# Four edits to a two-layer encoder on one core: ring tiles for the first weights behind the product pairs, later loads of stored tiles, another order inside each pair, a priority for the additions

## The chip, the core and the metric

The kernel runs on one core of a Trainium2 chip. The core's engines are named as in the profile: PE (TensorE, matmuls), DVE (VectorE), ACT (ScalarE), POOL (GpSimd) and SP (SyncE, which only issues transfers). The metric is the device time of one execution in microseconds (us); the times are medians over several runs.

## The reference

Two layers work on a sequence of 512 tokens with 16 meta tokens put ahead of them, 528 rows (`T`) of 2048 features, all in fp32. The first layer mixes by grouped-query softmax attention, the second by gated linear attention (GLA) in chunks, in both directions. Each has a gate path, and norms on both sides:

```
h = concat([meta, x])
for i in range(2):
    y = rmsnorm(h, pre_norm[i])
    y = attention_mixer(y, ...) if i == 0 else gla_mixer(y, ...)   # ends in (o * silu(gate)) @ w_out
    h = h + rmsnorm(y, post_norm[i])
return h[:, 16:]
```

Most of the arithmetic is in products with weights: `w_in` of the attention layer (2048 x 6144), its `w_out` (2048 x 2048), and the same two of the GLA layer.

## The kernel before

**Layout.** Activations lie with features on the 128 partitions and tokens along the free axis: 16 tiles (`KT`) of 128 features by 528 tokens. An output tile is 128 columns of a weight matrix by 528 tokens, computed as two halves of 264 tokens (`HALF`). An fp32 product is made of three: each operand is split into a high part (a cast) and a low part (what is left), and high x high, high x low and low x high are added up in PSUM (`three`, L152 to L155). The activations' parts are `uh` and `ul`.

**Weights.** `weights` (L141) loads a unit of 1024 columns (8 k tiles of 128 x 128) into a raw tile `wraw`, of which there are two, by SP's queue (L148). `split` then casts it on ACT (L130) and subtracts on DVE (L131) into a pair of tiles `whi` and `wlo`, a ring of three. A call may bring its own pair of tiles instead (`own`). `project` (L157) multiplies two such units, 48 matmuls for each half tile, and hands the bank to an `evac` function.

**Pairs.** `seven` (L213) computes two output tiles together with seven products instead of eight, in Strassen's manner: the weights for two tiles are a 2 x 2 block of quarters a11, a12, a21, a22 (1024 columns each, loaded at L219 by SP's queue), and the activations were combined ahead into `th`, `tl` (by `combine`) with four columns T1 to T4. Each product is 24 matmuls (L239 to L241). Sums of quarters are made on DVE (L232), every operand is split into ring tiles (`parts`), results are copied from PSUM on ACT (L268, L270, L272, L280) and partial results are added to what is there on DVE (`add`, L247). Six raw tiles pass through a list `free`: the two `wraw` and four others; a pair returns the list in the order in which the next shall use it. Pairs make up the attention gates (5 pairs, in 106 to 215 us), eight tiles of the attention's output product (4 pairs, in 813 to 895 us) and the GLA values (6 pairs, in 1042 to 1173 us).

**Behind the output product's pairs.** The output tiles 0 to 12 are stored to `y_d` as they come. When the last pair is done, its pools are closed, and a pool `tp` takes their space: in it lie the 16 tiles `hs`, the three pairs `own`, and tiles for a small product of the next layer (`wr`, loaded at L856, and `wl`, which is cleared on POOL at L858 and cast from `wr` on ACT). POOL issues the loads of 13 stored tiles (L851). Then come the last three output tiles, 13, 14 and 15 (`TAIL`): first the left half of each, then the right half, with the same split weights (`kept`, six units: tile 13 with k 0 to 7, tile 13 with k 8 to 15, then 14 and 15 likewise). The first three units go to `own` tiles, the last three to the ring. `squares` copies each half to `hs` (L868), squares it on ACT (L870) and adds the squares up on POOL (L872). From the sums `mean_rsqrt` makes a row, with which `residual` (L893 to L898) makes the next layer's input on DVE and ACT; the first product of the next layer (L982, weights `w_in1`) follows, with transposes of `hs` (L935) between its matmuls.

**What sets the order.** A scheduler puts the instructions on each engine in order, by the order in which they are written and by priorities: a block in `tc.high_priority(n)` counts as written n steps earlier (`AHEAD` for weights and sums, `AHEAD + 200` for the quarters' loads). `clk` is an aid for the writing: `clk.after(dt, fn)` calls `fn` when products worth dt us have been written. It makes nothing wait on the chip. Each engine then runs its list in that order.

Of the kernel before, what the change touches and what calls it, by code (L numbers as in the profile page):

```python
# [11 lines left out]
F32R = mybir.dt.float32r  # L12
I32 = mybir.dt.int32
AF = mybir.ActivationFunctionType
ALU = mybir.AluOpType
# [4 lines left out]
P = 128  # L20
# [14 lines left out]
AHEAD = 400  # L35
# [47 lines left out]
def hybrid_encoder(  # L83
# [5 lines left out]
    nc = tc.nc  # L89
    V, A, G, PE = nc.vector, nc.scalar, nc.gpsimd, nc.tensor  # L90
    clk = Clock()

    def pool(stack, name, bufs=1, **kw):
        return stack.enter_context(tc.tile_pool(name=name, bufs=bufs, reuse_waits="tile", **kw))
# [13 lines left out]
    y_d = scratch.tile([13, P, T], F32, name="y_d")  # L108
# [20 lines left out]
    def split(hi, lo, src):  # L129
        A.copy(hi, src)  # L130
        V.tensor_tensor(lo, src, hi.bitcast(F32), op=ALU.subtract)  # L131
# [10 lines left out]
    def weights(src, ahead=AHEAD, queue=nc.sync, own=None):  # L142
        n = src.shape[-1]
        with tc.high_priority(ahead):
            raw = wpool.tile([P, 1024], F32, tag="wraw", name="wraw", bufs=2)
            hi, lo = own or (wpool.tile([P, 1024], F32R, tag="whi", name="whi"),
                             wpool.tile([P, 1024], F32R, tag="wlo", name="wlo"))
            queue.dma_start(out=raw.rearrange("p (k n) -> p k n", n=n), in_=src)  # L148
            split(hi, lo, raw)
        return hi.rearrange("p (k n) -> p k n", n=n), lo.rearrange("p (k n) -> p k n", n=n)  # L150
# [40 lines left out]
    T1, T3, T4, T2 = range(0, 4 * HALF, HALF)  # L191
# [23 lines left out]
    def seven(src, c, ys, th, tl, free, ps_x):  # L215

        def quarter(t, i, j):
            with tc.high_priority(AHEAD + 200):
                nc.sync.dma_start(out=t.rearrange("p (k n) -> p k n", n=P),  # L219
                                  in_=src[:, j * KH:(j + 1) * KH, c + i * P:c + (i + 1) * P])  # L220
            return t

        def parts(raw):
            with tc.high_priority(AHEAD):
                hi = wpool.tile([P, 1024], F32R, tag="whi", name="whi")
                lo = wpool.tile([P, 1024], F32R, tag="wlo", name="wlo")
                split(hi, lo, raw)
            return [t.rearrange("p (k n) -> p k n", n=P) for t in (hi, lo)]

        def sums(o, a, b, op=ALU.subtract):  # L230
            with tc.high_priority(AHEAD):
                V.tensor_tensor(o, a, b, op=op)  # L232

        def product(w, b, ps=None, more=False):
            if ps is None:
                ps = ps_x.tile([P, 512], F32, tag="x", name="px")[:, :HALF]
            bh, bl = b
            for k in range(KH):
                PE.matmul(ps, w[0][:, k], bh[:, k], start=k == 0 and not more, stop=False, skip_group_check=more)  # L239
                PE.matmul(ps, w[0][:, k], bl[:, k], start=False, stop=False, skip_group_check=more)  # L240
                PE.matmul(ps, w[1][:, k], bh[:, k], start=False, stop=k == KH - 1,  # L241
                          skip_group_check=more)
                clk.step(3 * (HALF + 7) / 2400)
            return ps

        def add(o, ps, y):
            V.tensor_tensor(o, ps, y, op=ALU.add)  # L247

        def of_u(j, n):
            a, b = HALVES[n]  # L250
            return [t[:, j * KH:(j + 1) * KH, a:b] for t in (uh, ul)]

        def of_t(o):
            return [t[:, :, o:o + HALF] for t in (th, tl)]
        a11, a21, a22, s, a12, spare = free
        for t, i, j in ((a11, 0, 0), (a21, 1, 0), (a22, 1, 1), (a12, 0, 1)):
            quarter(t, i, j)
        y1, y2 = ys
        l, r = slice(0, HALF), slice(HALF, T)
        w1 = parts(a11)  # L260
        sums(s, a21, a22, ALU.add)
        w5 = parts(s)
        sums(a21, a11, a21)
        sums(a11, s, a11)
        w2 = parts(a11)
        p1 = ps_p.tile([P, 512], F32, tag="pp", name="pp")[:, :HALF]
        product(w1, of_u(0, 0), p1)
        A.copy(y1[:, l], p1)  # L268
        p5 = product(w5, of_t(T1))
        A.copy(y2[:, r], p5)  # L270
        product(w2, of_t(T2), p1, True)
        A.copy(y1[:, r], p1)  # L272
        add(y1[:, l], product(parts(a12), of_u(1, 0)), y1[:, l])
        sums(a11, a12, a11)
        product(parts(a21), of_t(T3), p1, True)
        add(y2[:, r], p1, y2[:, r])
        product(parts(a11), of_u(1, 1), p5, True)
        add(y1[:, r], p5, y1[:, r])
        product(parts(a22), of_t(T4), p1, True)
        A.copy(y2[:, l], p1)  # L280
        return [spare, s, a21, a11, a12, a22]

    w_in0 = attn_w_in[0].rearrange("(k p) n -> p k n", p=P)
    w_out0 = attn_w_out[0].rearrange("(k p) n -> p k n", p=P)
# [262 lines left out]
    for h in range(3):  # L547
        y = yp.tile([P, T], F32, tag=f"y{h % 2}", name="y")
# [258 lines left out]
    def y_tile(i):  # L807
        return yp.tile([P, T], F32, tag=f"y{i}", name=f"y{i}")
# [19 lines left out]
    for m in range(2, 5):  # L828
        y = y_tile(m % 2)
# [17 lines left out]
    tp = pool(tr, "tp")  # L847
    t2 = pool(tr, "t2", 2)
    hs = [tp.tile([P, T], F32, name=f"h{k}") for k in range(KT)]
    for m in range(KT - 3):  # L850
        nc.gpsimd.dma_start(out=hs[m], in_=y_d[m])  # L851
    r0 = tp.tile([P, T], F32, name="r0")


# [86 lines left out]
    turn, spare = [0], [True]  # L941
# [27 lines left out]
                    clk.after(3.2 + t, lambda k=k, t=t: token_major(k - 3, t))  # L969
            yield 0.6  # L970

    own = [[tp.tile([P, 1024], F32R, name=f"own{i}{w}") for w in "hl"] for i in range(3)]
    kept = {}
    for part in HALVES:
        for m in range(KT - TAIL, KT):
            if m not in kept:
                kept[m] = [weights(w_out0[:, k0:k0 + 8, m * P:(m + 1) * P], own=own.pop(0) if own else None)
                           for k0 in (0, 8)]
            project(w_out0, m * P, (part,), evac, ws=kept[m])
    clk.finish(*side)  # L980
# [447 lines left out]
    y = [fp.tile([P, D], F32, name=f"y{t}") for t in range(4)]  # L1428
# [75 lines left out]
```

## Time and profile before

| | |
|---|---|
| median of 3 runs | 1802.85 us (1802.39 to 1803.79) |
| the profiled execution | 1801.52 us |
| its span in the trace | 1799.8 us |
| mean granted clock of TensorE | 0.993 |
| PE busy | 1749.2 us, 97% |
| DVE, ACT, POOL busy | 65%, 54%, 18% |
| PE busy in 106 to 215 us (attention gates) | 105.57 of 109 us |
| PE busy in 813 to 895 us (output pairs) | 82.00 of 82 us |
| PE busy in 895 to 930 us (last three tiles, left and right halves) | 24.58 of 35 us |
| PE busy in 1042 to 1173 us (GLA values) | 128.85 of 131 us |

A window gives, for a stretch of the execution, each engine's busy time and its count of instructions (x), the clock that TensorE was granted, the share of time that the 16 DMA engines were busy, and their rate. A row of a timeline gives the start, the duration, engine, line, operation and tiles, and in brackets the idle time ahead of it with what ended it. All times in the trace are from the start of the span.

### The profile page before, as it was taken

To read this page: it belongs to the slowest core of one execution; us is meant where nothing else is said; L and a number is where in the kernel's file an instruction comes from. 1 tells how busy PE (TensorE), PEld (TensorE's weight loads), DVE (VectorE), ACT (ScalarE), POOL (GpSimd) and SP (SyncE) were. 2 spreads that over 40 slices of the span, in tenths; PEclk is the share of its full clock that TensorE was granted. 3 is DMA by queue.
4 is the path that set the end of the run, shared out by engine and by line. 5 is a ranking of instruction groups with operands and counts; after the bars stand their busy time and mean duration, and the time that the engine had idled before them with its cause. 6 is when DMAs were issued, how large, how long until landed. Compare 5 with 4: busy or idle time off the path is not lost. (4 is left out here: it accounts for less than half of the span.)

```text
span 1799.8 us, 31575 instructions
## 1 busy us (share of the span) xinstructions
PE 1749.2 (97%) x12495; PEld 1647.1 (92%) x12495; DVE 1177.0 (65%) x1913; ACT 978.2 (54%) x1957; POOL 319.5 (18%) x416
## 2 busy tenths in 40 slices
PE   8999999899999999999989999999999999999998
PEld 7999999899999999999989899988898989888886
DVE  4878676666676676776638876668585766764224
ACT  5644455556556455544427544468685765853221
POOL 3124014322422322141221101110000100000000
PEclk9999999999999999999989999999999999999999
DMA  8444423223233233363456444343242332354333
GB/s 251 141 132 122 127 78 101 83 84 107 80 87 101 73 89 107 126 196 113 122 170 207 119 129 119 95 130 107 78 117 72 113 90 85 96 154 176 94 94 129
DMA packets 268068, 211.22 MB, mean 117 GB/s; under 512 B 10284, under 2 KB 240368, under 8 KB 267392
## 3 DMA queue, kind: packets, MB, share of 16 engines
q1 hardware_dynamic: 251600, 159.00, 31.0%
q0 software_dynamic: 16320, 50.21, 8.2%
q8 instruction: 98, 1.61, 0.4%
q14 instruction: 50, 0.41, 0.1%
HBM read 171.15 MB, written 31.52 MB: 113 GB/s over the span
## 5 line engine op out<-in xcount | busy, mean ns | idle before, releaser
L153 PE MATMUL pp<-uh,whi 128*128 128x264 f32 (+1 forms) x2064 | 641.8, 311 | 5.8 <-ACT whi L130 5.2
L155 PE MATMUL pp<-uh,wlo 128*128 128x264 f32 (+1 forms) x2064 | 632.0, 306 | 2.0 <-DVE wlo L131 1.6
L154 PE MATMUL pp<-ul,whi 128*128 128x264 f32 (+1 forms) x2064 | 631.3, 306 | 2.2 <-DVE ul L442 2.2
L131 DVE TENSOR_TENSOR wlo<-wraw,whi 128x1024 fp32r<-128x1024 f32 (+1 forms) x233 | 286.3, 1229 | 245.8 <-ACT whi L130 244.2
L153 PEld LDWEIGHTS pp<-uh,whi 128*128 128x128 f32 x2064 | 390.7, 189 | 22.5 <-ACT whi L130 5.5
L155 PEld LDWEIGHTS pp<-uh,wlo 128*128 128x128 f32 x2064 | 390.6, 189 | 19.6 <-DVE wlo L131 2.4
L154 PEld LDWEIGHTS pp<-ul,whi 128*128 128x128 f32 x2064 | 391.4, 190 | 16.0 <-DVE ul L442 2.6
L130 ACT CAST whi<-wraw 128x1024 fp32r<-128x1024 f32 (+1 forms) x233 | 242.6, 1042 | 274.1 <-PE f L1416 83.4
L130 ACT CAST whi<-x 128x1024 fp32r<-128x1024 f32 x57 | 59.8, 1049 | 71.3 <-PE pp L240 25.4
L131 DVE TENSOR_TENSOR wlo<-x,whi 128x1024 fp32r<-128x1024 f32 x57 | 73.5, 1290 | 35.3 <-ACT whi L130 35.3
L310 POOL DMA_DIRECT2D qs<-qw x96 | 48.3, 508 | 252.1 <-ACT sq L304 215.7
L662 ACT ACTIVATE pn<-s,mx 128x528 f32<-128x528 f32 (+1 forms) x72 | 50.1, 696 | 48.6 <-DVE mx L659 48.6
L1416 PE MATMUL f<-whi,ul 128*128 128x512 f32 x192 | 75.6, 394 | 0.0
L1414 PE MATMUL f<-whi,uh 128*128 128x512 f32 x192 | 75.5, 393 | 0.0
L1415 PE MATMUL f<-wlo,uh 128*128 128x512 f32 x192 | 75.3, 392 | 0.0
L659 DVE TENSOR_REDUCE mx<-s 128x1 f32<-128x528 f32 (+1 forms) x72 | 50.6, 703 | 28.0 <-PE s L656 27.4
L239 PE MATMUL px<-uh,whi 128*128 128x264 f32 x240 | 68.4, 285 | 0.0
L241 PE MATMUL px<-uh,wlo 128*128 128x264 f32 x240 | 68.3, 284 | 0.0
L240 PE MATMUL px<-ul,whi 128*128 128x264 f32 x240 | 67.9, 283 | 0.0
L677 DVE TENSOR_TENSOR pl<-pT,ph 128x512 fp32r<-128x512 f32 (+1 forms) x80 | 47.3, 591 | 18.9 <-ACT ph L676 18.3
L676 ACT CAST ph<-pT 128x512 fp32r<-128x512 f32 (+1 forms) x80 | 40.8, 509 | 31.0 <-PE pT L672 24.9
L1260 POOL DMA_DIRECT2D og_d<-og x24 | 12.9, 542 | 186.2 <-DVE og L1258 186.2
(472 smaller groups left out, 4253.1 us busy)
## 6 DMA issues: line engine op xcount, KB each, us to landing
wraw<-in_attn_w_in_dram SPq DMA_DIRECT2D x80, 512.0 KB, 4.0
wraw<-in_gla_w_in_dram SPq DMA_DIRECT2D x80, 512.0 KB, 4.0
wraw<-in_gla_w_out_dram SPq DMA_DIRECT2D x32, 512.0 KB, 3.9
wraw<-in_attn_w_out_dram SPq DMA_DIRECT2D x22, 512.0 KB, 4.1
x<-in_gla_w_in_dram SPq DMA_DIRECT2D x16, 512.0 KB, 4.2
x<-in_attn_w_in_dram SPq DMA_DIRECT2D x14, 512.0 KB, 4.3
qs<-qw POOLq DMA_DIRECT2D x96, 66.0 KB, 4.0
x<-h_d SPq DMA_DIRECT2D x32, 132.0 KB, 2.9
```

What stands on the lines that cost most here:

```text
L130: A.copy(hi, src)
L131: V.tensor_tensor(lo, src, hi.bitcast(F32), op=ALU.subtract)
L153: PE.matmul(ps, wh, uh[:, k, a:b], start=first, stop=False)
L154: PE.matmul(ps, wh, ul[:, k, a:b], start=False, stop=False)
L155: PE.matmul(ps, wl, uh[:, k, a:b], start=False, stop=last)
L239: PE.matmul(ps, w[0][:, k], bh[:, k], start=k == 0 and not more, stop=False, skip_group_check=more)
L240: PE.matmul(ps, w[0][:, k], bl[:, k], start=False, stop=False, skip_group_check=more)
L241: PE.matmul(ps, w[1][:, k], bh[:, k], start=False, stop=k == KH - 1, skip_group_check=more)
L659: V.reduce_max(mx, s, axis=AX.XY, negate=True)
L1414: PE.matmul(ps, uh[:, k, ts], wh[:, kk], start=(k == 0), stop=False)
L1415: PE.matmul(ps, uh[:, k, ts], wl[:, kk], start=False, stop=False)
L1416: PE.matmul(ps, ul[:, k, ts], wh[:, kk], start=False, stop=(k == KT - 1))
```

## The change: what it does

1. `add` (L247) runs in `tc.high_priority(AHEAD + 100)`: ahead of splits and sums that are written in the same place, behind the quarters' loads.
2. In `seven` the quarters are loaded in the order a11, a12, a21, a22 (before: a11, a21, a22, a12). The plain product of a12 with `uh` comes second, with its addition right behind it; the product with T1, which opens the bank p5, goes from second to fourth, with its copy. The split of a12 (`w6`) stands right behind that of a11. The list for the next pair is returned in another order.
3. The loads of the 13 stored tiles are no longer written at once but at 6.0 + 1.25 m us of written products.
4. The first three units of the last three tiles use the ring, the last three the `own` tiles.

One line more in `add` moves every later line number up by one.

```
         def add(o, ps, y):
-            V.tensor_tensor(o, ps, y, op=ALU.add)
+            with tc.high_priority(AHEAD + 100):
+                V.tensor_tensor(o, ps, y, op=ALU.add)
...
-        for t, i, j in ((a11, 0, 0), (a21, 1, 0), (a22, 1, 1), (a12, 0, 1)):
+        for t, i, j in ((a11, 0, 0), (a12, 0, 1), (a21, 1, 0), (a22, 1, 1)):
             quarter(t, i, j)
         y1, y2 = ys
         l, r = slice(0, HALF), slice(HALF, T)
         w1 = parts(a11)
+        w6 = parts(a12)
         sums(s, a21, a22, ALU.add)
-        w5 = parts(s)
         sums(a21, a11, a21)
         sums(a11, s, a11)
         w2 = parts(a11)
         p1 = ps_p.tile([P, 512], F32, tag="pp", name="pp")[:, :HALF]
         product(w1, of_u(0, 0), p1)
         A.copy(y1[:, l], p1)
-        p5 = product(w5, of_t(T1))
-        A.copy(y2[:, r], p5)
+        add(y1[:, l], product(w6, of_u(1, 0)), y1[:, l])
         product(w2, of_t(T2), p1, True)
         A.copy(y1[:, r], p1)
-        add(y1[:, l], product(parts(a12), of_u(1, 0)), y1[:, l])
+        p5 = product(parts(s), of_t(T1))
+        A.copy(y2[:, r], p5)
         sums(a11, a12, a11)
         product(parts(a21), of_t(T3), p1, True)
...
-        return [spare, s, a21, a11, a12, a22]
+        return [spare, a21, a12, a11, s, a22]
...
     for m in range(KT - 3):
-        nc.gpsimd.dma_start(out=hs[m], in_=y_d[m])
+        clk.after(6.0 + 1.25 * m, lambda m=m: nc.gpsimd.dma_start(out=hs[m], in_=y_d[m]))
...
-    own = [[tp.tile([P, 1024], F32R, name=f"own{i}{w}") for w in "hl"] for i in range(3)]
+    own = [None] * 3 + [[tp.tile([P, 1024], F32R, name=f"own{i}{w}") for w in "hl"] for i in range(3)]
...
-                kept[m] = [weights(w_out0[:, k0:k0 + 8, m * P:(m + 1) * P], own=own.pop(0) if own else None)
+                kept[m] = [weights(w_out0[:, k0:k0 + 8, m * P:(m + 1) * P], own=own.pop(0))
```

How the order moves is seen in the engines' lists. First ACT, from the end of the last pair of the output product on: `y` are the pair's results, `whi` ring tiles, `h` and `sq` the evacuation of a half tile. Before:

```order
L280 COPY y_10706<-pp 128x264
L816 ACTIVATE sq<-y_10706 128x528
L130 CAST own0h<-wraw 128x1024
L130 CAST own1h<-wraw 128x1024
L130 CAST own2h<-wraw 128x1024
L130 CAST whi<-wraw 128x1024
L868 COPY h_10950<-pp 128x264
L870 ACTIVATE sq<-pp 128x264
L130 CAST whi<-wraw 128x1024 x2
L868 COPY h_10951<-pp 128x264
L130 CAST wl<-wr 128x16x16 x2
```

The same place after the change:

```order
L130 CAST whi<-wraw 128x1024 x2
L817 ACTIVATE sq<-y_10705 128x528
L130 CAST whi<-wraw 128x1024
L281 COPY y_10706<-pp 128x264
L817 ACTIVATE sq<-y_10706 128x528
L130 CAST own0h<-wraw 128x1024
L130 CAST own1h<-wraw 128x1024
L130 CAST wl<-wr 128x16x16 x2
L869 COPY h_10950<-pp 128x264
L871 ACTIVATE sq<-pp 128x264
L130 CAST own2h<-wraw 128x1024
```

Three casts of the tail's weights now stand ahead of the last pair's last copy (L281), and the two casts of `wl` have moved ahead of the first half tile's evacuation and of the cast for own2.

POOL at the same place, from the last addition of the pairs' squares on, before (`h_10937` to `h_10949` are the 13 stored tiles; ten of the rows are left out here):

```order
L817 TENSOR_TENSOR acc<-acc,sq 128x528
L851 DMA h_10937<-y_d 128x528
L851 DMA h_10938<-y_d 128x528
...
L851 DMA h_10949<-y_d 128x528
L856 DMA wr<-in_gla_w_in_dram 128x16x32
L858 MEMSET wl 128x2048
L872 TENSOR_TENSOR acc<-acc,sq 128x264 x4
```

After, with rows left out in the same way:

```order
L818 TENSOR_TENSOR acc<-acc,sq 128x528
L857 DMA wr<-in_gla_w_in_dram 128x16x32
L859 MEMSET wl 128x2048
L852 DMA h_10937<-y_d 128x528
L852 DMA h_10938<-y_d 128x528
L852 DMA h_10939<-y_d 128x528
L873 TENSOR_TENSOR acc<-acc,sq 128x264
L852 DMA h_10940<-y_d 128x528
...
L852 DMA h_10944<-y_d 128x528
L873 TENSOR_TENSOR acc<-acc,sq 128x264
L852 DMA h_10945<-y_d 128x528
...
```

The load of `wr` and the clearing of `wl` now come first, and the stored tiles' loads follow in three runs of 3, 5 and 5 with additions between them.

DVE in the second attention pair, whose results are `y_1519` and `y_1520` (`x_751` to `x_754` are raw tiles of the list `free`), before:

```order
L232 TENSOR_TENSOR x_754<-wraw,x_752 128x1024
L247 TENSOR_TENSOR y_1519<-px,y_1519 128x264
L232 TENSOR_TENSOR wraw<-x_751,wraw 128x1024
L131 TENSOR_TENSOR wlo<-wraw,whi 128x1024
L247 TENSOR_TENSOR y_1520<-pp,y_1520 128x264
```

After:

```order
L248 TENSOR_TENSOR y_1519<-px,y_1519 128x264
L131 TENSOR_TENSOR wlo<-wraw,whi 128x1024
L131 TENSOR_TENSOR wlo<-x_754,whi 128x1024
L536 SCALAR_TENSOR_TENSOR sq<-ssq,erow 128x264
L232 TENSOR_TENSOR x_754<-wraw,x_752 128x1024
L232 TENSOR_TENSOR wraw<-x_751,wraw 128x1024
L131 TENSOR_TENSOR wlo<-x_753,whi 128x1024
L248 TENSOR_TENSOR y_1520<-pp,y_1520 128x264
```

The first addition has moved ahead of the next pair's sums by several steps; the second still stands behind two sums and a split. In the first GLA pair, `tl<-x_12144,th`, the low part of the last but one step of `combine`, has moved ahead of one sum and one split of DVE; the tile `x_12144` is the one into which a12 is loaded, before and after.

More of the change, by code (lines that the diff above doesn't have):

```diff
@@ L246, in add @@
         def add(o, ps, y):
-            V.tensor_tensor(o, ps, y, op=ALU.add)
+            with tc.high_priority(AHEAD + 100):
+                V.tensor_tensor(o, ps, y, op=ALU.add)
         def of_u(j, n):
@@ L255, in seven @@
         a11, a21, a22, s, a12, spare = free
-        for t, i, j in ((a11, 0, 0), (a21, 1, 0), (a22, 1, 1), (a12, 0, 1)):
+        for t, i, j in ((a11, 0, 0), (a12, 0, 1), (a21, 1, 0), (a22, 1, 1)):
             quarter(t, i, j)
@@ L260, in seven @@
         w1 = parts(a11)
+        w6 = parts(a12)
         sums(s, a21, a22, ALU.add)
-        w5 = parts(s)
         sums(a21, a11, a21)
@@ L268, in seven @@
         A.copy(y1[:, l], p1)
-        p5 = product(w5, of_t(T1))
-        A.copy(y2[:, r], p5)
+        add(y1[:, l], product(w6, of_u(1, 0)), y1[:, l])
         product(w2, of_t(T2), p1, True)
         A.copy(y1[:, r], p1)
-        add(y1[:, l], product(parts(a12), of_u(1, 0)), y1[:, l])
+        p5 = product(parts(s), of_t(T1))
+        A.copy(y2[:, r], p5)
         sums(a11, a12, a11)
@@ L280, in seven @@
         A.copy(y2[:, l], p1)
-        return [spare, s, a21, a11, a12, a22]
+        return [spare, a21, a12, a11, s, a22]
     w_in0 = attn_w_in[0].rearrange("(k p) n -> p k n", p=P)
@@ L850, in hybrid_encoder @@
     for m in range(KT - 3):
-        nc.gpsimd.dma_start(out=hs[m], in_=y_d[m])
+        clk.after(6.0 + 1.25 * m, lambda m=m: nc.gpsimd.dma_start(out=hs[m], in_=y_d[m]))
     r0 = tp.tile([P, T], F32, name="r0")
@@ L970, in residuals @@
             yield 0.6
-    own = [[tp.tile([P, 1024], F32R, name=f"own{i}{w}") for w in "hl"] for i in range(3)]
+    own = [None] * 3 + [[tp.tile([P, 1024], F32R, name=f"own{i}{w}") for w in "hl"] for i in range(3)]
     kept = {}
@@ L976, in hybrid_encoder @@
             if m not in kept:
-                kept[m] = [weights(w_out0[:, k0:k0 + 8, m * P:(m + 1) * P], own=own.pop(0) if own else None)
+                kept[m] = [weights(w_out0[:, k0:k0 + 8, m * P:(m + 1) * P], own=own.pop(0))
                            for k0 in (0, 8)]
```

## The prediction, made before the changed kernel was run

> **What bounds the kernel now.** I read the page first, then windows of 10 us for TensorE, then its waits, and only at the places with a gap the timelines and the DMA views. The page's head and its row for TensorE:
>
> ```profile
> span 1799.8 us, 31575 instructions
> PE 1749.2 (97%) x12495; PEld 1647.1 (92%) x12495; DVE 1177.0 (65%) x1913; ACT 978.2 (54%) x1957; POOL 319.5 (18%) x416
> ```
>
> PE is the bound, so only its stops and its slow clock can be won; the number of matmuls does not change. The windows (x is the count of matmuls, the last three numbers are granted clock, DMA share, GB/s):
>
> ```profile
> 885.00:895.00 10.00, 10.00 (x85) 10.00 (x84) 3.64 (x5) 1.83 (x3) 1.58 (x2) 1.00 0.42 124
> 895.00:905.00 10.00, 6.75 (x42) 6.33 (x41) 3.18 (x5) 2.90 (x4) 7.45 (x13) 0.83 0.65 198
> 905.00:915.00 10.00, 6.51 (x37) 5.88 (x35) 1.23 (x1) 1.05 (x1) 4.60 (x5) 0.83 1.08 354
> 915.00:925.00 10.00, 6.31 (x35) 6.01 (x36) 3.16 (x3) 4.15 (x8) 1.15 (x1) 0.66 0.50 120
> 909.20:912.60 3.40, 3.40 (x18) 3.40 (x17) 0.00 (x0) 0.00 (x0) 2.98 (x2) 0.50 1.07 344
> 145.00:155.00 10.00, 7.72 (x63) 7.53 (x62) 9.45 (x10) 3.94 (x7) 4.78 (x3) 1.00 0.26 82
> ```
>
> A full window holds 85. From 895 to 925 there are 42 + 37 + 35 = 114 where 255 would fit: 141 matmuls are missing, and at 10/85 us each that is 16.6 us. This is the passage from the last pair to the three half tiles. The table of TensorE's waits (total us, times, longest) names what it waits for there and elsewhere:
>
> ```profile
> PE pp L153 <- ACT whi L130: 5.2, 1, 5.2
> PE pp L239 <- DVE y L247: 2.9, 2, 2.3
> PE px L239 <- ACT th L130: 2.1, 1, 2.1
> PE pp L153 <- ACT own0h L130: 2.1, 1, 2.1
> PE ht L935 <- DVE h L896: 1.3, 2, 1.1
> PE pp L155 <- DVE own0l L131: 1.1, 1, 1.1
> PE pp L155 <- DVE own2l L131: 0.8, 1, 0.8
> PE pp L153 <- ACT own2h L130: 0.7, 1, 0.7
> PE px L241 <- DVE wlo L131: 0.4, 1, 0.4
> ```
>
> The tail's own waits (own0, own2, the single whi) are 5.2 + 2.1 + 1.1 + 0.8 + 0.7 = 9.9 us; the other 6.7 of the 16.6 is mainly matmuls at half clock behind those stops. One such stretch is the 3.4 us row above: 18 matmuls instead of 29 cost 11 x 10/85 = 1.3 us.
>
> **The tail, edits 3 and 4.** ACT's and POOL's timelines and the DMA view of 895 to 920 (queues, then issues with count, KB each, median us to landing):
>
> ```profile
> 896.57 1.03 ACT L130 CAST own0h<-wraw 128x1024 fp32r<-128x1024 f32 x1
> 906.17 1.05 ACT L130 CAST own2h<-wraw 128x1024 fp32r<-128x1024 f32 x1 [7.62 <-DMA wraw<-in_attn_w_out_dram]
> 917.14 1.04 ACT L130 CAST whi<-wraw 128x1024 fp32r<-128x1024 f32 x1 [9.92 <-DMA wraw<-in_attn_w_out_dram]
> 924.62 0.71 ACT L130 CAST wl<-wr 128x256 fp32r<-128x256 f32 x2
> ...
> 896.82 1.31 POOL L817 TENSOR_TENSOR acc<-acc,sq 128x528 f32<-128x528 f32 x1
> 898.07 5.47 POOL L851 DMA_DIRECT2D h<-y_d  x10
> 909.33 1.17 POOL L856 DMA_DIRECT2D wr<-in_gla_w_in_dram  x1 [0.34 <-DMA h<-y_d]
> ...
> q0 software_dynamic: 1234, 4.12, 50.7%
> q1 hardware_dynamic: 3120, 1.57, 23.4%
> ...
> h<-y_d POOLq DMA_DIRECT2D x13, 264.0 KB, 7.7
> wraw<-in_attn_w_out_dram SPq DMA_DIRECT2D x4, 512.0 KB, 8.4
> wr<-in_gla_w_in_dram POOLq DMA_DIRECT2D x1, 256.0 KB, 7.7
> ```
>
> Two things hold the half tiles up. The first unit's cast (own0h) stands behind the last pair's end, as its tile lies in the space that the pair's tiles leave; and ten loads issued in 5.47 us fill the DMA engines, so that weights land in 8.4 us. The page has the quiet value of the same loads, the PE and DVE timelines the pace of the last pair:
>
> ```profile
> wraw<-in_attn_w_out_dram SPq DMA_DIRECT2D x22, 512.0 KB, 4.1
> ...
> 892.46 0.28 PE L239 MATMUL pp<-sh,whi 128*128 128x264 f32 x1
> ...
> 895.24 0.28 PE L241 MATMUL pp<-sh,wlo 128*128 128x264 f32 x1
> ...
> 887.79 1.23 DVE L131 TENSOR_TENSOR wlo<-wraw,whi 128x1024 fp32r<-128x1024 f32 x1 [0.53 <-ACT whi L130]
> ```
>
> The seventh product's 24 matmuls start from 892.46 to 895.24: 0.121 us each, 2.9 a product, so the fifth ends at 889.6, the sixth at 892.5, the seventh at 895.4. A unit of a half tile is also 24 matmuls, so from 895.4 on units are needed every 2.9 us: 895.4, 898.3, 901.2, 904.1, 907.0, 909.9. A split is a cast of 1.05 and a subtraction of 1.23, 2.3 together. With the ring for the first three, unit 1 needs a ring tile (free at 889.6) and is ready near 892. Unit 2's raw tile is free when the subtraction of 887.79 ends, 889.0; with 4.1 it lands at 893.1 and is ready at 895.4, 2.9 early. Unit 3 uses the raw tile of unit 1: issued near 892, landed 896, ready 898.4, 2.8 early. Unit 4 (own0) is issued at 895.4, ready 901.8, 2.3 early; unit 5 (own1) at 898.4, ready 904.8, 2.2 early. Unit 6 (own2) is issued at 901.8 and would be ready at 908.2, but its cast now stands behind the two wl casts and an evacuation's two steps on ACT. POOL issues wr from 898.1 (end of the addition of 896.82) to 899.3; landing in 7.7 gives 907.0, the casts 907.7, the evacuation about 0.8 more, own2h at 908.5 to 909.6 and own2l to 910.8. Its third matmul, the first with the low part, is due at 909.9 + 0.24: a stop of about 0.6. Bounds: none, if wr lands in 4.1 as the quiet loads do; if own2's load takes 8.4, it lands at 910.2 and is ready at 912.5, a stop of 2.4 and one slow stretch of 1.3, 3.7. I take 0.6, since wr's row is its own. Tail: 16.6 - 0.6 = 16.0 gained (12.9 to 16.6). The wl split and the memset, now early on POOL, wait for nothing that PE needs. The thirteen stored tiles leave POOL in runs of 3, 5 and 5 between additions, not singly; the first three run beside the load of own0 or own1, which have 2.2 to spare.
>
> [...]
>
> The clock: after stops of 0.7 and 0.8 the row of 909.2 shows 0.50; in 145 to 155, with a longest stop of 2.3, it stays 1.00. So one stop of 0.6 may or may not cost 1.3; the sum takes nothing, the bound takes it. [...]
>
> **The pairs, edits 1 and 2.** In the second attention pair the seventh product waits for the addition that reads its bank:
>
> ```profile
> 143.84 2.01 DVE L232 TENSOR_TENSOR wraw<-x,wraw 128x1024 f32<-128x1024 f32 x1
> 145.78 2.33 DVE L131 TENSOR_TENSOR wlo<-wraw,whi 128x1024 fp32r<-128x1024 f32 x1
> 148.02 0.42 DVE L247 TENSOR_TENSOR y<-pp,y 128x264 f32<-128x264 f32 x1
> ```
>
> The attention stops are 2.9 + 0.4 = 3.3 us. In the new order the addition still stands behind two sums and one split; only the 0.4 of the plain product's addition has gone from between. The raised priority would win all 3.3 only if loads landed so early that the order did not matter. I take the middle of 0.4 and 3.3: 1.8 gained. The other pairs, but for the first of the GLA layer (below), are not among these waits, so they can only lose; their weights keep coming through the same raw tiles at 4.1, and I take 0.
>
> The first GLA pair has the stop on th (2.1). The plain product needs no th, so this goes; but it needs a12, whose tile the last step of combine frees:
>
> ```profile
> 1041.51 1.26 DVE L131 TENSOR_TENSOR tl<-x,th 128x1056 fp32r<-128x1056 f32 x1
> ...
> 1045.32 0.38 ACT L268 COPY y<-pp 128x264 f32<-128x264 f32 x1 [2.06 <-PE pp L241]
> 1048.53 1.05 ACT L130 CAST whi<-x 128x1024 fp32r<-128x1024 f32 x1 [2.83 <-DMA x<-in_gla_w_in_dram]
> ```
>
> Now the tile is free at 1042.8 and its load ends near 1048.5: 5.7. In the new order that subtraction stands ahead of one sum and one split, 2.3 earlier (1.23 and about 1.05): free at 1040.5, landed at 1044.6 (4.1) to 1046.2 (5.7), split until 1046.9 to 1048.5. The second product is due at 1045.3, its low part at 1045.6: a new stop of 1.3 to 2.9, taken as 2.1. Net 0 (-0.8 to +0.8).
>
> **Behind the tail** the residuals make PE wait 1.3 (ht). With the tail 16 us shorter, two splits of w_in1 (1.23 each on DVE) may fall ahead of that chain: 0 taken, bounds -1.3 to +2.5.
>
> Sum: -16.0 - 1.8 + 0 + 0 = -17.8. The profiled execution took 1801.52 us (span 1799.8), so 1783.7; the median of the runs, 1802.85, is 1.33 above it: **1785.1**. All best ends: -16.6 - 3.3 - 0.8 - 1.3 = -22.0, 1780.9. All worst: -12.9 - 0.4 + 0.8 + 2.5 = -10.0, 1792.9.
>
> **Rivals.** *Weights still crowded* (chance 0.13): all three own loads take 8.4. Own0 lands at 903.8, ready 906.1: 1.7 late; own1 lands 906.8, ready 909.1, 0.4 late; own2 waits for own0's raw tile, issued 906.1, lands 914.5, ready 916.8, 4.5 late. With two slow stretches 1.7 + 0.4 + 4.5 + 2.6 = 9.2 instead of 0.6: 1793.7. For it: the loads of stored tiles still come in runs, and wr joins them. Against: 3 tiles, not 10, stand ahead of own0's landing.
>
> *Given back behind the tail* (0.10): the two splits delay the residuals by 2.5 and the stop slows the clock once, 1.3: +3.8, 1788.9.
>
> *Slower* (0.04): in each of the 15 pairs the addition, now pinned early on DVE, holds back the splits and sums behind it until its product ends, and so the raw tiles and next loads. It turns slower from 17.8/15 = 1.2 us a pair. DVE is busy 65%, 1.9 us of a product's 2.9, so about 1 us a product is to spare; a hold of one product less that, 1.9 a pair, gives 15 x 1.9 - 17.8 = +10.7, 1813.6. Against: additions wait for a product that is next to end anyway, and 885 to 895, the end of a pair, is full with the same three additions in it.
>
> *No change* (0.01): the first half tile stays behind the pair's end because ring and raw tiles come no sooner. The times above speak against it by 2 us.
>
> **How the numbers follow.** The forecast has 0.72, and its two faster rivals 0.23; what a measurement here can tell from no change is 0.2%, 3.6 us, and all three lie further below. Faster 0.95, same 0.01, slower 0.04. The range runs from the best end, 1780, to 1793, which holds the forecast's worst end and the second rival and leaves most of the first outside.
>
> **What would show it.** Right: 895 to 905 holds 85 matmuls, own0h is cast before it is needed, PE has no wait over 1 us on own tiles, and the clock stays 1.00; the next stage starts 16 us sooner. In the first GLA pair the stop moves to the second product. Wrong: loads of weights that take 8 us between 895 and 915, a wait on own2h of several us, or full windows turning to 80 inside the pairs.

## The result and the profile after

The changed kernel takes 1786.34 us (median of 4 runs, 1783.37 to 1787.44) against 1802.62 us for the kernel before (4 runs): the ratio is 0.9911 with a 95% interval of 0.9891 to 0.9931, 16 us less, by the interval 12 to 20. The forecast was 1785.1. The profiled execution took 1787.44 (span 1785.7).

The windows of the changed kernel over the tail, and over the second attention pair, in the columns of those shown of before:

```profile
895.00:905.00 10.00, 10.00 (x84) 10.00 (x84) 7.17 (x6) 4.66 (x7) 7.33 (x7) 1.00 0.81 228
905.00:915.00 10.00, 8.09 (x65) 7.67 (x64) 4.27 (x6) 3.91 (x8) 5.50 (x10) 1.00 0.96 307
915.00:925.00 10.00, 10.00 (x80) 9.87 (x81) 2.32 (x4) 3.12 (x6) 3.01 (x6) 1.00 0.69 231
145.00:155.00 10.00, 8.21 (x55) 8.00 (x54) 9.45 (x10) 3.74 (x6) 4.67 (x4) 0.83 0.26 82
```

From 895 to 925 there are now 84 + 65 + 80 = 229 matmuls where there were 114, and the clock stays at 1.00. One stop is left, in the second row. (The first 2.7 us of the first row still belong to the last pair, which ends at 897.7 now and ended at 895.4 before.) The attention pair's window has become worse: 55 for 63, at a clock of 0.83. TensorE's waits in the whole execution name both:

```profile
PE pp L239 <- DVE y L248: 2.7, 3, 1.8
PE px L241 <- DVE wlo L131: 1.9, 3, 0.8
PE pp L153 <- ACT own2h L130: 1.2, 1, 1.2
PE ht L936 <- DVE h L897: 1.1, 1, 1.1
PE pp L155 <- DVE own2l L131: 0.7, 1, 0.7
```

The waits on own0 (2.1 and 1.1), on the ring tile (5.2) and on th (2.1) are gone. Where the time went is seen from the length of the stages, from the first matmul of a stage to the first of the next (in the pairs, to 0.12 us behind the start of the last matmul), in us, worked out from the starts in the traces:

| kernel | attention pairs | to the output pairs | output pairs | tail, to the first GLA pair | GLA pairs | rest |
|---|---|---|---|---|---|---|
| before | 108.2 | 598.9 | 81.7 | 146.8 | 130.4 | 627.2 |
| the change | 109.9 | 599.3 | 82.6 | 131.9 | 130.0 | 626.2 |
| ring order alone | 107.8 | 600.4 | 82.6 | 139.2 | 130.4 | 627.4 |
| later loads alone | 108.5 | 600.7 | 83.6 | 139.0 | 131.5 | 627.0 |
| both edits of the tail | 108.2 | 602.5 | 81.9 | 130.8 | 130.2 | 627.5 |
| both edits of the pairs | 110.1 | 602.7 | 81.7 | 144.9 | 129.6 | 626.4 |
| the change, fold copied on ACT | 109.3 | 599.0 | 81.7 | 129.5 | 130.0 | 626.5 |
| the change, rotation of the first head group left out | 103.5 | 600.2 | 81.7 | 129.5 | 129.7 | 626.4 |

The second stage, which no edit of the first seven touches, shows how far two profiles differ by themselves: 598.9 to 602.7. Between before and the change the tail gave 14.9 us, the rest behind GLA 1.1 and the GLA pairs 0.4; 0.8 came ahead of the first pair, and attention took back 1.8, the output pairs 1.0 and the stretch between them 0.4: together 14.1, the difference between the two profiled executions.

### The profile page after: what moved, and what is told of

The parts are those of the page before. It is cut to its first block, busy times and chain, and to the rows that moved or that the text cites. A ratio compares the mean times of both kernels' runs of the same rounds, so it can differ in the third digit from the quotient of the medians.

```text
span 1785.7 us, 31568 instructions
## 1 busy us (share of the span) xinstructions
PE 1745.8 (98%) x12495; PEld 1643.6 (92%) x12495; DVE 1182.2 (66%) x1913; ACT 978.6 (55%) x1957; POOL 319.5 (18%) x416
## 4 chain that ended last, share of the span: by engine, by line
PE 69%; DVE 4%; ACT 2%; DMA 2%; issue 1%; POOL 1%; DVEq 0%; ACTq 0%; POOLq 0%; SPq 0%
PE pp L153 12%; PE pp L155 12%; PE pp L154 12%; PE f L1417 2%; PE f L1415 2%; PE f L1416 2%; PE pp L239 2%; PE pp L240 2%; PE pp L241 2%; PE px L241 1%; PE px L239 1%; PE px L240 1%; PE pT L673 1%; DVE wlo L131 1%; DMA wraw<-in_attn_w_out_dram 1%
## 5 line engine op out<-in xcount | busy, mean ns | idle before, releaser
L131 DVE TENSOR_TENSOR wlo<-wraw,whi 128x1024 fp32r<-128x1024 f32 (+1 forms) x230 | 280.4, 1220 | 231.6 <-ACT whi L130 230.0
L241 PEld LDWEIGHTS px<-uh,wlo 128*128 128x128 f32 x240 | 45.1, 188 | 2.5 <-DVE wlo L131 2.5
## 6 DMA issues: line engine op xcount, KB each, us to landing
x<-h_d SPq DMA_DIRECT2D x32, 132.0 KB, 2.8
```

## The experiments

**The tail's two edits, apart and together.** Ring order alone:

```
-    own = [[tp.tile([P, 1024], F32R, name=f"own{i}{w}") for w in "hl"] for i in range(3)]
+    own = [None] * 3 + [[tp.tile([P, 1024], F32R, name=f"own{i}{w}") for w in "hl"] for i in range(3)]
...
-                kept[m] = [weights(w_out0[:, k0:k0 + 8, m * P:(m + 1) * P], own=own.pop(0) if own else None)
+                kept[m] = [weights(w_out0[:, k0:k0 + 8, m * P:(m + 1) * P], own=own.pop(0))
```

> Kernel before with the ring order alone (first three units of the last three tiles in ring tiles, last three in own tiles; the 13 stored tiles still loaded at once). Theory A (ring order and later loads each carry a part): the stop of 2.4 at the pair's end and the 1.4 and slow stretch behind it go (some 5 us), but own tiles loaded among the 13 loads land in 8 us or more, so a wait on own tiles of 4 to 8 us and a slow stretch stay: 6 to 10 us faster than before, near 1794. Rival B (the ring order alone is the gain, the loads do not matter): 15 us faster, no wait over 2 us on own tiles.

Measured: 1796.5 us, ratio 0.9961 (0.9947 to 0.9975). Later loads alone:

```
-        nc.gpsimd.dma_start(out=hs[m], in_=y_d[m])
+        clk.after(6.0 + 1.25 * m, lambda m=m: nc.gpsimd.dma_start(out=hs[m], in_=y_d[m]))
```

> Kernel before with the later loads of the stored tiles alone (own tiles still first). Theory A: the stop at the pair's end (2.4 and 1.4, with a slow stretch of 1.3) stays, the waits on own2 and on the ring tile behind it shrink from 7.5 us to under 2: 8 to 11 us faster, near 1793. Rival B: within 2 us of before. Rival C (crowding is the whole loss): 15 us faster.

Measured: 1797.36 us, ratio 0.9966 (0.9952 to 0.9981). Both:

> Kernel before with both edits of the tail (ring order and later loads), pairs and additions as before. Theory A, from the stages of the two profiles: the tail gains 15 us by itself and the pairs' edits have lost about 2, so this is faster than the full change: 15 to 17 us under before, 1 to 3 us under the full change. Rival D (the pairs' new order is what frees the raw tiles early enough for the ring): 5 us or more of the gain are missing here.

Measured: 1787.7 us, ratio 0.9908 (0.9893 to 0.9923). TensorE's waits from the last pair's end on, first of the ring order alone, then of the later loads alone:

```profile
PE pp L153 <- ACT own2h L130: 6.2, 1, 6.2
PE pp L155 <- DVE own2l L131: 0.4, 1, 0.4
```

```profile
PE pp L153 <- ACT own0h L130: 2.1, 1, 2.1
PE pp L155 <- DVE wlo L131: 1.4, 2, 0.8
PE pp L155 <- DVE own0l L131: 1.1, 1, 1.1
PE pp L155 <- DVE own2l L131: 0.7, 1, 0.7
PE pp L153 <- ACT own2h L130: 0.7, 1, 0.7
```

With both edits the 30 us from the last pair's end hold no stop:

```profile
898.00:928.00 30.00, 30.00 (x246) 29.87 (x245) 13.30 (x20) 12.90 (x23) 15.49 (x21) 1.00 0.86 269
```

Each edit takes away the stops that belong to it: the ring those on own0 at the pair's end, the later loads the long one behind own2. Each shortens the tail by 8 us, and both by 16: the two add up. Theory A holds for the stops and the stages, with the ring order at the edge of its 6 to 10 by the medians (6.3 us) and the later loads below their 8 to 11 (5.5 us); the waits left on own2 and the ring tile there are 2.8 us together and not under 2. Rivals B and C fall. Rival D falls too, since the old pairs feed the ring as well. One part of theory A missed: this kernel was to be 1 to 3 us under the full change, and its ratio of 0.9908 cannot be told from the full change's 0.9911. So by the times edits 1 and 2 add nothing to the two edits of the tail and take nothing from them.

**The pairs' edits by themselves** (the changed kernel with the two edits of the tail undone).

> The full change without the two edits of the tail: pairs in the new order and additions first, the last three tiles and the loads as before. Theory A: 0 to 3 us slower than before: attention pairs up to 2 slower by a stop and a slow stretch, output pairs 1 slower, first GLA pair 0.5 faster. Rival D: 3 us or more faster, as forecast for attention or more.

Measured: 1801.11 us, ratio 0.9988 (0.9979 to 0.9997), 0.5 to 3.8 us faster, where theory A had 0 to 3 slower. Rival D misses too. The profiled execution is the longest of the eleven (1804.37) and 2.9 longer than that of before; 3.8 more went into the stretch between attention and output pairs, which the edits do not touch. Its stages show a loss and a gain: attention is slower, 110.1 against 108.2, as with all edits, while the GLA pairs and what is behind them are 1.6 faster. Another 1.9 lies in the tail, where this kernel's loads are those of before; whether that comes of the pairs' order is not shown, as a later kernel with the old pairs and the old tail (rotation on DVE, below) has 1.0 less than before there as well. Edit 1 has no part in it by itself: in the kernel before, with that edit alone, every engine's order is as it was, since the additions did not stand where a priority moves them.

**The stop that was left on own2.** In the changed kernel DVE, POOL, ACT and SP show these rows around it:

```profile
900.57 4.33 DVE L866 COPY fold<-ident 64x64 f32<-64x64 f32 x2
905.05 1.23 DVE L131 TENSOR_TENSOR own0l<-wraw,own0h 128x1024 fp32r<-128x1024 f32 x1
...
900.55 1.32 POOL L818 TENSOR_TENSOR acc<-acc,sq 128x528 f32<-128x528 f32 x1
901.83 1.19 POOL L857 DMA_DIRECT2D wr<-in_gla_w_in_dram  x1
903.01 1.83 POOL L859 MEMSET wl<- 128x2048 f32 x1
...
902.09 1.05 ACT L130 CAST own0h<-wraw 128x1024 fp32r<-128x1024 f32 x1 [1.69 <-DMA wraw<-in_attn_w_out_dram]
906.73 0.72 ACT L130 CAST wl<-wr 128x256 fp32r<-128x256 f32 x2 [0.71 <-DMA wr<-in_gla_w_in_dram]
912.48 1.04 ACT L130 CAST own2h<-wraw 128x1024 fp32r<-128x1024 f32 x1 [4.47 <-DMA wraw<-in_attn_w_out_dram]
...
906.30 0.37 SPq L148 DMA_DIRECT2D wraw<-in_attn_w_out_dram  x1
```

ACT's cast of own2 waited for its load, not for the casts of wl, which were done 5 us earlier. The load was issued at 906.30, when own0's subtraction had freed the raw tile; and that subtraction, whose cast was done at 903.1, stood until 905.05 behind two copies of 64 x 64 that took 4.33 us. They end where POOL's clearing ends (904.90 and 904.84). The load itself took 6.2 us, where those of own0 and own1 took 4.3. An estimate from these rows: with the subtraction right behind its cast, or with a landing in 4.1, 0.3 or less of the 1.9 us would be left, so the late issue and the slow landing made this stop together. The experiment makes these copies on ACT:

```
-        V.tensor_copy(fold[r:r + 64], ident[r:r + 64, r:r + 64])
+        A.copy(fold[r:r + 64], ident[r:r + 64, r:r + 64])
```

> The full change with one edit: the two 64 x 64 copies of fold are made on ACT and not on DVE. Theory F (in the full change these copies took 4.3 us on DVE beside POOL's addition, transfer issue and clearing, held the subtraction of own0 by 1.9 us and so the raw tile and the load of own2): own0's subtraction follows its cast at once, own2 is issued 1.9 us earlier, the waits on own2 (1.2 and 0.7) fall under 0.5 together, the stretch from the last pair's end to the first GLA pair takes 130 us and not 131.9; 2 us less in all, at the edge of what the times can tell. Rival W (the casts of wl ahead of own2's cast are the cause, as forecast): the stop stays, since wl's casts stay where they are. Rival H (own2's load is slow beside the stored tiles): own2 is issued earlier, but lands 6 us after its issue or later, and half of the stop stays.

Measured: 1783.91 us, ratio 0.9891 (0.9877 to 0.9904), by the medians 2.4 under the full change; the two intervals overlap, so the times alone do not tell these kernels apart, but the trace does. Its rows for own0l, own2h and the 30 us behind the last pair:

```profile
901.54 1.23 DVE L131 TENSOR_TENSOR own0l<-wraw,own0h 128x1024 fp32r<-128x1024 f32 x1 [2.83 <-ACT own0h L130]
...
907.75 1.05 ACT L130 CAST own2h<-wraw 128x1024 fp32r<-128x1024 f32 x1 [1.68 <-DMA wraw<-in_attn_w_out_dram]
...
895.50:925.50 30.00, 30.00 (x246) 29.87 (x245) 13.22 (x21) 13.95 (x26) 15.82 (x21) 1.00 0.86 274
```

No stop is left, the tail takes 129.5 us instead of 131.9, and the casts of wl stand where they stood: theory F holds and rival W falls. Own2 was issued 1.6 us earlier behind the pair's end and landed in 5.0, so rival H falls in this run. The other test puts wr's load, the clearing and the casts later:

```
-    nc.gpsimd.dma_start(out=wr, in_=w_in1[:, :, 6144:6176])
...
+    def low_weights():
+        nc.gpsimd.dma_start(out=wr, in_=w_in1[:, :, 6144:6176])
...
+    clk.after(22.0, low_weights)
```

> The full change with the load of wr, the clearing of wl and its split written 22 us later, so that neither wl's casts nor the clearing come ahead of own2, and six stored tiles are issued in a row in their place. Theory F with the clearing as holder: fold's second copy no longer takes 3 us; both together 0.4 to 1.5. If transfer issues on POOL hold DVE's copy too, they take 3 us and more. Rival W: with wl's casts out of the way own2's stop is gone. Rival H: with six stored tiles beside them own1 and own2 land in 6 us or more, and the stop stays or grows.

Measured: 1792.62 us in a single run; the tail took 135.0. Rows of DVE, POOL, SP and ACT, as above:

```profile
903.35 1.42 DVE L869 COPY fold<-ident 64x64 f32<-64x64 f32 x2
...
903.34 1.37 POOL L818 TENSOR_TENSOR acc<-acc,sq 128x528 f32<-128x528 f32 x1
904.66 3.21 POOL L852 DMA_DIRECT2D h<-y_d  x6
...
907.09 0.37 SPq L148 DMA_DIRECT2D wraw<-in_attn_w_out_dram  x1
...
915.35 1.04 ACT L130 CAST own2h<-wraw 128x1024 fp32r<-128x1024 f32 x1 [5.91 <-DMA wraw<-in_attn_w_out_dram]
```

The copies now end with POOL's addition (904.77 and 904.71), so they are short, as theory F has it. Whether the clearing alone held the long copy is not settled: that copy began at 901.94, while POOL was issuing wr's load (901.83 to 903.01), and no copy on DVE in the other profiles begins inside an issue. But own2's load, issued 6.5 us behind the last pair's end (900.55), landed 8.3 us after its issue, beside stored tiles that left POOL six in a row, and TensorE waited 1.2 and 0.7 for it again, with wl's casts out of the way: rival W falls once more, and rival H holds here. An issue at 8.6 behind the pair's end with a landing of 6.2 is late (the changed kernel), one at 6.5 with 8.3 is late, one at 7.0 with 5.0 is not (fold on ACT).

How near this is to chance, a later run shows. The kernel whose rotation is left out in the attention pairs (below) has the changed kernel's tail, with fold on DVE, and no stop in it. DVE and POOL there:

```profile
894.82 1.42 DVE L867 COPY fold<-ident 64x64 f32<-64x64 f32 x2
...
894.80 1.38 POOL L819 TENSOR_TENSOR acc<-acc,sq 128x528 f32<-128x528 f32 x1
```

The first copy took 0.18 here and the second waited for the end of the addition. In the changed kernel's profile the first waited for it (1.36), and the second was then held until the clearing's end (2.95). Both began within 0.02 us of POOL's addition. So the two copies on DVE cost 1.4 or 4.3 us, with starts that differ by hundredths of a microsecond; on ACT they cost 0.5, and none of the five kernels that have them there waits for an own tile.

**The attention pairs.** The changed kernel, without the three elementwise operations on POOL in the first head group:

```
-        G.tensor_tensor(qw, qw, cos, op=ALU.mult)
...
+        if turn:
+            G.tensor_tensor(qw, qw, cos, op=ALU.mult)
...
```

> The full change without the three elementwise operations on POOL that turn q and k of the first head group during the attention pairs (the rotation is left out there, the four transfers stay). Theory P (two sums and a split on DVE take 2.2 us beside POOL and 1.2 without, and the addition behind them holds the seventh product): the operations take 1.2, the stop at the second attention pair falls from 2.1 to under 0.5, attention pairs take 107 to 108 us and not 109.9. Rival L (the landing of the raw tile sets it): the operations get shorter but the stop stays over 1 us.

Measured: 1779.3 us in a single run; attention pairs 103.5 us against 109.9, where 107 to 108 were expected. DVE and POOL at the second pair in the changed kernel, then DVE without the rotation:

```profile
143.04 2.24 DVE L232 TENSOR_TENSOR wraw<-x,wraw 128x1024 f32<-128x1024 f32 x1
145.21 2.34 DVE L131 TENSOR_TENSOR wlo<-x,whi 128x1024 fp32r<-128x1024 f32 x1
147.47 0.42 DVE L248 TENSOR_TENSOR y<-pp,y 128x264 f32<-128x264 f32 x1
...
144.16 2.31 POOL L313 TENSOR_TENSOR qs<-qs,sin 128x528 f32<-128x528 f32 x1
```

```profile
141.81 1.23 DVE L232 TENSOR_TENSOR wraw<-x,wraw 128x1024 f32<-128x1024 f32 x1
142.95 1.22 DVE L131 TENSOR_TENSOR wlo<-x,whi 128x1024 fp32r<-128x1024 f32 x1
144.08 0.42 DVE L248 TENSOR_TENSOR y<-pp,y 128x264 f32<-128x264 f32 x1
```

The same operations take half the time, the addition is done at 144.5 and TensorE never waits there: theory P. Rival L falls. So what held the seventh product was DVE beside POOL, not the order. That asks for another place for these operations. In the next two runs DVE makes them, first for the first head group, then for all; fold stays on ACT. The edit of the second run:

```
-    def rotate(qw, qs):
+    def rotate(qw, qs, E=V):
...
-        G.tensor_tensor(qw, qw, cos, op=ALU.mult)
+        E.tensor_tensor(qw, qw, cos, op=ALU.mult)
...
```

> The full change with fold copied on ACT and the first head group's three elementwise operations of the rotation on DVE and not on POOL. Theory P (POOL's operations make DVE's beside them take 2.2 us and not 1.2): attention pairs 103.5 to 105 us and not 109.3, no stop over 1 us in them, three operations of some 0.7 us added on DVE for each of three groups; 5 us under the same kernel with POOL, near 1779, the fastest so far. Rival S (DVE has no room for 6 us more in these 104 us): stops of 1 to 2 us at the additions stay, under 2 us gained.

Measured: 1782.74 us (1780.25 to 1787.62), ratio 0.9892 (0.9872 to 0.9912). Attention pairs take 105.7 us, 3.6 less than with the rotation on POOL, and TensorE's waits in them are 0.3 us at most, but the median fell by only 1.2 where 5 were expected, within the scatter: the stretch behind it was 2.4 longer in this profile.

> As the run before, with the rotation of all head groups on DVE. Theory P: the stretch between the attention pairs and the output pairs, 599 us, gains only where DVE holds PE up: 0 to 3 us. Rival S: DVE is fuller there and the stretch gets up to 4 us longer.

Measured: 1769.86 us (1768.68 to 1771.25), ratio 0.9817 (0.9801 to 0.9832): 33 us under before and the clear best so far. The expectation had 0 to 3 us for the stretch between attention and output pairs; it gave 11.6, from 599.0 with fold on ACT alone to 587.4. There the window of 330 to 450, each time with TensorE's wait on vt in the whole execution, first with the rotation on POOL, then on DVE:

```profile
330.00:450.00 120.00, 114.47 (x934) 113.65 (x933) 79.72 (x154) 69.14 (x153) 34.19 (x41) 0.99 0.32 92
PE vps L600 <- ACT vt L595: 7.3, 4, 4.8
```

```profile
330.00:450.00 120.00, 119.28 (x988) 118.49 (x987) 90.33 (x174) 71.03 (x159) 17.48 (x28) 1.00 0.32 92
PE vps L600 <- ACT vt L595: 0.7, 1, 0.7
```

DVE is busier (90.33 for 79.72), and still TensorE has 54 matmuls more; the wait on vt, the largest of all in the profile of before, is 0.7. Two stretches of 3.4 us at half clock, which the stage had with the rotation on POOL, are gone as well: the granted clock of the windows 330 to 450 and 690 to 814 was 0.99 there and is 1.00. That wait looked like one for ACT. At its longest, with the rotation on POOL and in the last row on DVE, the traces show:

```profile
345.61 1.32 POOL L312 TENSOR_TENSOR qw<-qw,cos 128x528 f32<-128x528 f32 x1 [4.80 <-DMA qs<-qw]
350.06 1.34 POOL L643 TENSOR_TENSOR gs<-gs,gr 128x528 f32<-128x528 f32 x1
354.19 0.71 DVE L633 TENSOR_TENSOR gr<-gr,rrow 128x528 f32<-128x528 f32 x1 [6.22 <-DMA gr<-g_d]
360.63 0.69 PE L600 MATMUL vps<-ident,vt 128*128 128x128 f32 x2 [4.79 <-ACT vt L595]
...
342.74 1.32 POOL L643 TENSOR_TENSOR gs<-gs,gr 128x528 f32<-128x528 f32 x1 [1.39 <-ACT gs L140]
```

The multiplication of a gate (L643) stands on POOL behind the rotation, which waits for its own transfers first. ACT had the gate ready at 345.85; the multiplication began 4.2 us later. When it ended, at 351.40, SP issued the load of the next gate tile (351.43). DVE waited for that tile, ACT's next steps waited 6.97 us for DVE, and the copy of vt stands behind them on ACT. With the rotation on DVE the multiplication (last row) began 0.15 behind the end of ACT's work on the gate. DVE's splits take 1.22 us in this window in both kernels. So the order of POOL's list made this stop, and not DVE beside POOL as in the attention pairs. The shorter waits on vt were not followed.

Then the old order of the pairs with the rotation on DVE, once in the kernel before (first head group alone) and once with everything else of the fastest kernel:

> The kernel before with the first head group's rotation on DVE. Theory P: the old order of the pairs gains as much, attention pairs at 103.5 to 105 us and not 108.2; then the new order is worth nothing there in either case. Rival O (the new order helps once the contention is gone): 1 us or more longer than with the new order.

Measured: 1797.17 us in a single run; attention pairs 104.0 us against 105.7 with the new order. Rival O falls.

> The fastest kernel so far (both edits of the tail, fold copied on ACT, rotation on DVE everywhere) with the pairs in the order of before, that is without edits 1 and 2. Theory A (the new order of the pairs is worth nothing in attention and some 1.5 us in and behind the GLA pairs): attention pairs 104 us against 105, GLA pairs and the rest behind them 1 to 2 us longer, in all within 2 us of the same kernel with the new order, 1768 to 1772. Rival D (the new order is worth what was forecast, or the tail needs it): 3 us or more slower, with waits on own tiles.

Measured: 1770.8 us, ratio 0.9815 (0.9801 to 0.9828), the same as with the new order. Attention pairs take 104.0 (new order 105.0), the tail 129.5 (129.4), GLA pairs 132.0 (131.5), the rest 627.4 (625.9). Rival D falls once more. By the profiles the pairs' new order takes 1.0 in attention and gives 2.0 us behind; in the times it cannot be told from nothing.

**The new order in the GLA layer alone**, with the tail's edits and fold on ACT:

> Both edits of the tail, fold copied on ACT, and the new order of the pairs in the GLA layer alone (attention and output pairs in the order of before). Theory A: attention pairs 108.2 us (109.4 with one slow stretch), the tail 130.5 as with the tail's edits alone, GLA pairs 130 and the rest behind them 626: 3 us under the tail's edits alone by the span, 1 to 3 under the full change, near 1784. Rival D (the new order helps the tail by freeing raw tiles early): a wait on own tiles of 1 us or more comes back, no gain over the full change.

Measured: 1786.66 us, ratio 0.9908 (0.9894 to 0.9921), where 1784 was expected. Attention (108.6) and the GLA pairs (129.5) came out as expected, but the gain behind the GLA pairs did not: the rest took 627.7. The tail took 131.3, with no wait on an own tile, so rival D's sign is missing, though its forecast of no gain over the full change (0.9908 against 0.9911) came true. The stop in the rest, which is 1.5 us in the kernel before,

```profile
PE pz L1127 <- ACT z L1128: 1.5, 1, 1.5
```

is there in this run too (1.6) and in every kernel whose attention and output pairs have the old order (1.2 to 1.7); where all pairs have the new order it is 0.3 at most. So it hangs on the order of those earlier pairs and not on the GLA pairs' own. How was not found out.

## Why the prediction was right, point by point

- **The tail (16.0 forecast, 14.9 by the traces): right in its mechanism.** The ring carries the first three units and the loads no longer crowd the rest (own0 and own1 landed in 4.3 us and own2 in 6.2, where the median was 8.4 before); apart, the two edits show the two halves. The three units are ready 3.4 us ahead of the pair's end, at it and 2.9 us behind it, where the working gives 3.4, 0 and 3.0, and own0 and own1 are issued at it and 2.9 us behind it, where it gives 0 and 3.0. The row from 895 to 905 is full and the clock stays at 1.00, as was said. The 1.1 us that are missing lie in the next step.
- **The stop on own2 (0.6 forecast, 1.9 measured): the step failed.** It said that own2 is issued 6.4 us behind the pair's end, lands in 4.1 and then waits for the casts of wl. It was issued 8.6 us behind it (906.30 against 897.73), because fold's copies held own0's subtraction, and landed in 6.2; the casts of wl were done by then. Fold's copies, 0.39 us in the trace of before, were costed at nothing; they now begin together with POOL's work, and that they can stretch there was not seen.
- **Attention (-1.8 forecast, +1.8 measured): the step failed.** It took the middle between 0.4 and 3.3 without a row that spoke for it. The rows it quoted held the answer: a sum of 2.01 and a split of 2.33, where such operations take 1.23 elsewhere. The order could not remove the stop, as POOL set it: TensorE's waits in these pairs are 3.5 us, where they were 3.3. Of the loss, 1.3 is a stretch at half clock, which the old order also showed in the run with later loads alone.
- **Output pairs (0 forecast, +1.0 measured).** A stop of 0.9 us came at 873. The old order has such a stop in three of its profiles too (0.6 to 2.0), so it is not shown to belong to the change.
- **The first GLA pair (0 forecast, -0.4 measured over the six pairs): right.** The wait on th is gone, and in its place are two waits at the second product, 0.4 for the high part and 0.8 for the low part, 1.2 where 2.1 was taken:

```profile
PE px L241 <- DVE wlo L131: 0.8, 1, 0.8
PE px L239 <- ACT whi L130: 0.4, 1, 0.4
```

- **Behind the tail (0 forecast): right.** The wait on ht is 1.1, where it was 1.3. The 1.1 us behind the GLA pairs were in no step.
- **The sum** of 17.8 against 14.1 in the two profiled executions and 16.3 in the medians: the large term was right. The tail missed by 1.1, attention by 3.6, the output pairs by 1.0 and the stretch between them by 0.4; against these stand 2.3 us that no step had foreseen, 0.8 ahead of the first pair, 0.4 in the GLA pairs and 1.1 behind them. That the median came within 1.2 us of the forecast is in part luck.
- **The rivals.** Weights as crowded as before did come back, in the run with wr late, where six stored tiles were issued in a row and own2 landed in 8.3; in the changed kernel, with runs of 3 and 5, own0 and own1 landed in 4.3 and only own2, with 6.2, was slowed. The slower case did not come: the priority alone moves nothing.

## What to carry to other kernels

When weights are late at a seam between stages, look for two things at once: where the tiles lie that the first loads need, and what else is queued on the DMA engines; here each was worth half, and both were needed for a passage without a stop. Test the parts of a change apart: of the four edits here two carry the whole gain, and the order of the pairs is worth nothing that the times can show. When an operation takes 2.2 us in one place and 1.2 in all others, look at what runs beside it before the order is changed. And when an engine with little to do stands at the start of a chain, look at its list: three small operations moved from POOL, busy 18% of the span, to DVE, busy 66%, were worth 14 us here over all head groups, nearly as much as the whole change, part of it because DVE no longer ran beside them and part because POOL's next operation no longer stood behind them.

## What the runs showed of the hardware

**DVE beside POOL.** Fold's copies on DVE, 0.18 to 0.19 us each when undisturbed, ended with POOL's operation: at 904.90 beside a clearing that ended at 904.84, at 904.77 beside an addition that ended at 904.71, at 896.24 beside one that ended at 896.18, and with both edits of the tail

```profile
901.84 1.42 DVE L865 COPY fold<-ident 64x64 f32<-64x64 f32 x2
...
901.83 1.38 POOL L817 TENSOR_TENSOR acc<-acc,sq 128x528 f32<-128x528 f32 x1
```

at 903.26 and 903.21. In all four the last copy ended 0.05 to 0.06 us behind POOL's operation. In four profiles the first copy took its 0.18 although POOL's addition had begun 0.01 to 0.02 us earlier by the record, as in the row above, and the addition took 1.37 to 1.38, for 1.32 where the first copy waited: by these rows a recorded start does not tell which of the two came first. The larger operations, which stretched from 1.2 to 2.3 us next to POOL operations of 2.3, are longer than their own time by 1.0 to 1.1 us. POOL's operation of the same shape takes 1.32 where DVE makes no such sums and splits beside it (345.61 in the rows above), so it was longer by 1.0 too. How the two hold each other up, no run here shows.

**The clock.** After a stop of 2.07 us between two matmuls in the attention pairs the changed kernel ran 3.4 us at half clock; with both edits of the tail a longer stop at the same place, 2.63, had no such stretch (both from start to start). Windows of both just behind the stop:

```profile
148.90:152.30 3.40, 3.40 (x18) 3.40 (x17) 3.17 (x5) 1.79 (x3) 0.11 (x1) 0.51 0.52 153
```

```profile
147.70:151.10 3.40, 3.40 (x28) 3.40 (x29) 3.40 (x3) 0.95 (x2) 0.65 (x1) 1.00 0.56 159
```

So a stop of 2 to 3 us costs 1.3 us more in some executions and not in others: of the nine profiles with a stop of 2.0 to 3.1 us there, five have the stretch, and the length of the stop does not sort them. In the trace of before the stretches at half clock behind the last pair begin at 899.0, 909.2 and 916.0 and last 3.4, 3.4 and 6.8 us; the starts are 10.2 and 6.8 us apart, three and two times 3.4. What decides whether such a stretch follows a stop, no run here shows.
